# Masks of the prompt scores: from TensorE matmuls to VectorE additions, in the first of two attention stages

## The chip, the cores and the metric

The kernel runs on one core of a Trainium2 chip. The metric is device time of one execution in microseconds, the median of several runs. In what follows TensorE is the matrix engine, VectorE (DVE), ScalarE (ACT) and GpSimd (POOL) are the others that compute, and SyncE (SP) issues most DMAs.

## What is computed

One decoder layer, for a prompt of 1024 tokens and for 8 decode sequences of 8 tokens each. The mixing sub-layer has two head groups: differential attention (4 heads) and NSA, a native sparse attention (8 query heads on 2 key heads, with a compressed, a selected and a window branch). An MLP with squared ReLU follows. At these sizes all 16 blocks of 64 keys are selected in the prompt, so its selected branch is plain causal attention. What matters here is the masked softmax of the prompt:

```python
def masked_softmax(s, mask):
    s = jnp.where(mask, s.astype(jnp.float32), NEG)
    m = jnp.max(s, axis=-1, keepdims=True)
    p = jnp.where(mask, jnp.exp(s - m), 0.0)
    return p / jnp.maximum(jnp.sum(p, axis=-1, keepdims=True), 1e-30)

# nsa_attention: selected and window branches
smask = kpos <= tpos
wmask = (wpos[None, :] >= 0) & (dist >= 0) & (dist < WINDOW)     # WINDOW = 512
# diff_attention
p = masked_softmax(s, kpos[None, :] <= tpos[:, None])
```

## The kernel before

The prompt is cut into 8 tiles of 128 queries, and keys into blocks of 128. The program is one stream of Python calls without loops on the chip. It has these stages in order: input norm and the projections of compressed keys (`stage_keys`), NSA attention of the prompt (`stage_nsa`), differential attention of the prompt with the decode attention in between (`stage_diff`), the output projection, the MLP up and the MLP down.

`scores` (line 397) makes the probabilities of one query tile `i` against the key blocks `kb0` to `i`. Keys 0 to 511 and 512 to 1023 go to separate tiles `S` of 512 columns, one PSUM bank each. Each tile gets two matmuls (line 410), since the queries are split in a high and a low part (`ps`). Where the tile holds the diagonal block, a third matmul adds the diagonal mask (line 417): the identity `identb` in bf16 times the mask `m_diag`, 128 x 128. Where it holds the block at the far end of the window (only window heads, `sw == 1`, and `i >= 4`), another adds `m_far` (line 414). Then VectorE takes the maximum along the row (line 418), and the smaller of two where there are two tiles (line 422); ScalarE makes the exponentials with their sum (line 427). GpSimd scales the probabilities (line 481).

`stage_nsa` runs over 32 jobs: 2 key heads, 8 query tiles and 2 pairs of query heads. A job calls `scores` four times, twice for the selected and twice for the window branch (`nsa_scores`). In `nsa_values`, TensorE transposes the probabilities (line 517) into a PSUM tile `T`, which is copied to `pt` in SBUF, and multiplies them with the values (line 502). `merge` interleaves three lists by their stated costs: the values of the job before, the scores of this job, and fill work, which is the projections of later tiles (line 337). `stage_diff` is built in the same way, over 4 heads and 8 tiles, and calls the same `scores`.

In PSUM the NSA stage has four buffers for `S`, two for `T`, one for the output `o` and one for projections `M` (`PS_N`).

`evac` (line 141) chooses the engine of each copy from `T` to `pt`. `self.ld` holds an account of work in ns, `ld[0]` for ScalarE and `ld[1]` for VectorE. A copy of `n` columns would add 0.83 n + 60 to the first or 1.04 n + 70 to the second, and goes where the account is then lower. `scores` and other functions enter their own work in it. So line 139 (`act_copy`) is the copy on ScalarE and line 150 the one on VectorE. Semaphores and the final order of each engine's instructions are made by the tile framework at the end of the build.

Of the kernel before, what the change touches and what calls it, by code (L numbers as in the profile page):

```python
# [26 lines left out]
P = 128  # L27
# [40 lines left out]
def merge(*lists):  # L68

    lists = [l for l in lists if l]  # L70
    tot = [sum(c for c, _ in l) + 1e-9 for l in lists]
    done = [0.0] * len(lists)
    pos = [0] * len(lists)
    while True:
        best = None
        for n, l in enumerate(lists):
            if pos[n] < len(l):
                f = (done[n] + 0.5 * l[pos[n]][0]) / tot[n]
                if best is None or f < best[0]:
                    best = (f, n)  # L80
        if best is None:
            return
        n = best[1]
        c, fn = lists[n][pos[n]]
        fn()
        done[n] += c
        pos[n] += 1


def interleave(*lists):  # L90

    out = []
    merge(*[[(c, lambda i=i: out.append(i)) for i in l for c in [i[0]]] for l in lists])
    return out
# [31 lines left out]
class Kern:  # L126
# [270 lines left out]
    def scores(self, qs, j, kst, kc, i, kb0, sums, far):  # L397


        nc = self.nc  # L400
        segs = [(a, b) for a, b in ((kb0, min(i + 1, 4)), (max(kb0, 4), i + 1)) if a < b]
        nm = self.sm.tile([P, 2], F32, name="nm", bufs=8)
        tiles = []
        for n, (a, b) in enumerate(segs):
            hf = a // 4
            S = self.psum_s()
            lo = hf * 512
            far_here, diag_here = far and a <= kb0 < b, a <= i < b
            for ps in range(2):
                nc.tensor.matmul(S[:, a * P - lo:b * P - lo], qs[:, ps, j, :],  # L410
                                 kst[hf][:, kc, a * P - lo:b * P - lo],
                                 start=ps == 0, stop=ps == 1 and not (far_here or diag_here))
            if far_here:
                nc.tensor.matmul(S[:, kb0 * P - lo:(kb0 + 1) * P - lo], self.identb, self.m_far, start=False,
                                 stop=not diag_here)
            if diag_here:
                nc.tensor.matmul(S[:, i * P - lo:(i + 1) * P - lo], self.identb, self.m_diag, start=False, stop=True)  # L417
            nc.vector.reduce_max(nm[:, n:n + 1], S[:, a * P - lo:b * P - lo], axis=AX.X, negate=True)  # L418
            tiles.append(S)
            self.ld[1] += 1.04 * (b - a) * P + 66  # L420
        if len(segs) == 2:
            nc.vector.tensor_tensor(nm[:, 0:1], nm[:, 0:1], nm[:, 1:2], op=OP.min)  # L422
            self.ld[1] += 70
        p = self.pp.tile([P, 1024], F32, name="p")
        for n, (a, b) in enumerate(segs):
            lo = a // 4 * 512
            nc.scalar.activation(p[:, a * P:b * P], tiles[n][:, a * P - lo:b * P - lo], AF.Exp, bias=nm[:, 0:1],  # L427
                                 accum_out=sums[:, n:n + 1])
            self.ld[0] += 0.83 * (b - a) * P + 236
        return p  # L430
# [1349 lines left out]
    def fill_nsa(self):  # L1780
        self.kvs = [self.kv0, None]
        fill = self.nfill = Fill()
        sts = {}
        jobs = []
        late = []
        key = None
        kv1 = []
        for g in range(2):
            box = []
            fill.add([(0, lambda g=g, box=box: box.append(self.unit_q(g)))])  # L1790
            for t in [NT] + list(range(NT)) if g == 0 else list(range(NT)) + [NT]:
                st = sts[g, t] = {"g": g}
                items = self.lazy(lambda t=t, st=st, box=box: box[0](t, st), [660.0] * 4 + [10, 224])
                fill.add(interleave(items[:4], late))
                if key:
                    fill.mark(key)
                fill.add(items[4:5])
                late = items[5:]
                key = None
                if g == 0:  # L1800
                    kv1.append((t, self.lazy(lambda t=t: self.kv1_tile(t), [650.0] * 4 + [120])))
                    if t == 0:
                        fill.mark("pre")
                        fill.add([(0, self.kv1_open)])
                    if 1 < t < NT:
                        for _ in range(2 if t < 5 else 1):
                            fill.add(kv1.pop(0)[1])
                if t < NT:
                    late.append((110, lambda g=g, t=t: self.nsa_cmp_scores(g, t, sts[g, t])))
                    key = (g, t)  # L1810
                    jobs += [(g, t, 0), (g, t, 1)]
        fill.add(late)
        self.njobs, self.nsts = jobs, sts

    def stage_nsa(self):
        fill, jobs, sts = self.nfill, self.njobs, self.nsts
        prev = []
        merge(self.klate[:2])
        merge(fill.take(0, (0, 0)), self.klate[2:3])
        for n, (g, t, pr) in enumerate(jobs):  # L1820
            sc = self.nsa_scores(g, t, pr, sts[g, t])
            if n == 2:
                self.consts_late(self.bp)
            if n == 0:
                merge(sc, self.klate[3:])
                sc = []
            nxt = jobs[n + 1] if n + 1 < len(jobs) else None
            key = (nxt[0], nxt[1]) if nxt and nxt[2] == 0 else None
            bud = fill.left() / (len(jobs) - n)
            merge(prev, sc, fill.take(bud, key))  # L1830
            prev = self.nsa_values(g, t, pr, sts[g, t])
        self.tail = prev

    def stage_diff(self):
        fill = Fill()
        sts = {}
        jobs = []
        late = []
        heads = []
        for h in range(4):  # L1840
            weights, tile = self.unit_diff(h)
            for n, t in enumerate([NT] + list(range(NT))):
                st = sts[h, t] = {}
                items = self.lazy(lambda t=t, st=st, tile=tile: tile(t, st), [163.0 * 4] * 6 + [10, 224])
                if n == 0:
                    fill.add([(0, weights)])
                fill.add(interleave(items[:6], late + self.dec_slot(h, n)))
                fill.add(items[6:7])
                if jobs and late:
                    fill.mark(jobs[-1])  # L1850
                late = items[7:]
                if t < NT:
                    jobs.append((h, t))
        fill.add(late)
        fill.mark(jobs[-1])
        for n in range(36, 40):
            fill.add(self.dec_nsa_slot(n))
        prev = self.tail
        merge(prev, fill.take(0, (0, 0)))
        prev = []  # L1860
        for n, (h, t) in enumerate(jobs):
            sc = self.diff_scores(h, t, sts[h, t])
            key = jobs[n + 1] if n + 1 < len(jobs) else None
            bud = fill.left() / (len(jobs) - n)
            merge(prev, sc, fill.take(bud, key))
            prev = self.diff_values(h, t, sts[h, t])
        merge(prev, fill.take(1e12))
# [175 lines left out]
```

## Time and profile before

| | us |
|---|---|
| median of 3 runs | 1824.03 |
| lowest and highest | 1822.09, 1831.58 |
| the profiled execution | 1819.73 |
| its span, first to last instruction | 1817.9 |
| NSA stage of the prompt in it | about 172 to 545 |
| TensorE busy over the span | 1709.6 (94%) |
| VectorE busy | 1137.8 (63%) |
| ScalarE busy | 865.4 (48%) |

The profile is one execution, 4.3 us below the median of the runs. Durations and waits are read from it. Matmul rows overlap, and their ends are modelled, so a sum of their durations is more than the time that they take from the queue; the distance between two starts is what counts. A wait that is put down to an engine tells which semaphore came last. Masks in the NSA stage are the rows of lines 414 and 417 with `S<-maskb,identb`.

### The profile page before, as it was taken

How to read it: one execution, taken by the hardware profiler on the slowest of the kernel's cores; microseconds unless marked ns; L12 is line 12 of the kernel's file. 1: busy time of each engine (PE TensorE's matmuls, PEld its weight loads, DVE VectorE, ACT ScalarE, POOL GpSimd, SP SyncE). 2: the span in 40 equal slices, each digit the busy share in tenths (PEclk: the TensorE clock that was granted, in tenths of full speed). 3: DMA queues.
4: the chain of work that ended last, by engine and by line, in shares of the span. 5: the costliest groups of instructions: out<-in, count | busy, mean ns of one | idle time of the engine just before them, and what ended most of it. 6: DMA issues, size and time to landing. Idle time of an engine off the chain costs nothing. (4 is left out here: it accounts for less than half of the span.)

```text
span 1817.9 us, 33390 instructions
## 1 busy us (share of the span) xinstructions
PE 1709.6 (94%) x12155; PEld 1487.3 (82%) x12155; DVE 1137.8 (63%) x2716; ACT 865.4 (48%) x2188; POOL 273.3 (15%) x517
## 2 busy tenths in 40 slices
PE   7689999999998999999989997999999899999997
PEld 7678776677666778787877877999999899999996
DVE  5357667767863575667665478566666456847665
ACT  5244446456762364555555355444444334543442
POOL 1133335334330121212110000000000000000000
PEclk9888899999998999999998998999999999999999
DMA  7531000000203243424245322434443465554334
GB/s 195 115 75 45 14 14 24 7 4 23 58 7 113 86 145 88 120 81 130 65 134 182 129 91 80 140 133 151 145 145 110 159 214 168 177 165 115 106 118 150
DMA packets 193919, 191.92 MB, mean 106 GB/s; under 512 B 32562, under 2 KB 152986, under 8 KB 193754
## 3 DMA queue, kind: packets, MB, share of 16 engines
q1 hardware_dynamic: 191114, 185.10, 33.2%
q10 hardware_dynamic: 2640, 4.68, 0.8%
q8 instruction: 96, 1.57, 0.4%
q14 instruction: 69, 0.57, 0.1%
HBM read 133.75 MB, written 55.97 MB: 104 GB/s over the span
## 5 line engine op out<-in xcount | busy, mean ns | idle before, releaser
L337 PE MATMUL M<-w,xt 128*128 128x384 f32 (+4 forms) x1584 | 293.4, 330 | 15.4 <-ACT natk L139 12.6
L1665 PE MATMUL Dn<-hf,wf 128*128 128x272 f32 x2304 | 292.4, 290 | 10.1 <-ACT hf L139 8.1
L1665 PEld LDWEIGHTS Dn<-hf,wf 128*128 128x128 f32 x2304 | 291.0, 190 | 11.4 <-ACT hf L139 8.4
L337 PEld LDWEIGHTS M<-w,xt 128*128 128x128 f32 (+1 forms) x1584 | 243.8, 191 | 30.2 <-ACT natk L139 13.5
L427 ACT ACTIVATE p<-S,nm 128x512 f32<-128x512 f32 (+3 forms) x288 | 159.9, 561 | 87.8 <-DVE nm L422 48.8
L418 DVE TENSOR_REDUCE nm<-S 128x1 f32<-128x512 f32 (+3 forms) x288 | 148.1, 527 | 59.1 <-PE S L417 39.3
L175 POOL TENSOR_TENSOR rs_r<-rs_t,mhalf 128x1 f32<-128x1 f32 (+2 forms) x64 | 38.2, 599 | 955.1 <-DVE rs_t L173 952.2
L410 PE MATMUL S<-kst,qs 128*128 128x512 f32 (+3 forms) x576 | 162.1, 373 | 9.6 <-ACT p L427 8.6
L481 POOL TENSOR_SCALAR p<-p,coef 128x640 f32<-128x640 f32 (+7 forms) x128 | 92.5, 736 | 150.5 <-DVE coef L478 66.0
L410 PEld LDWEIGHTS S<-kst,qs 128*128 128x128 f32 x576 | 93.8, 194 | 22.6 <-ACT p L427 11.8
L1363 DVE TENSOR_TENSOR us<-ur,us 128x512 fp32r<-128x512 f32 x96 | 66.1, 691 | 66.2 <-ACT us L139 66.1
L139 ACT ACTIVATE us<-ur 128x512 fp32r<-128x512 f32 x101 | 63.4, 629 | 82.3 <-PE Uc L1437 50.4
L1437 PE MATMUL Ub<-xc,us 128*128 128x272 f32 x744 | 101.0, 288 | 0.0
L139 ACT ACTIVATE wf<-q 128x512 fp32r<-128x512 f32 x69 | 43.6, 632 | 116.5 <-PE Dn L1665 108.8
L1437 PE MATMUL Ua<-xc,us 128*128 128x272 f32 x744 | 99.0, 289 | 0.0
L150 DVE COPY pt<-T 128x512 f32<-128x512 f32 (+3 forms) x100 | 61.7, 618 | 55.9 <-PE T L517 42.1
L1437 PEld LDWEIGHTS Ub<-xc,us 128*128 128x128 f32 x744 | 96.1, 188 | 0.0
L1437 PEld LDWEIGHTS Ua<-xc,us 128*128 128x128 f32 x744 | 95.8, 189 | 0.0
L139 ACT ACTIVATE hf<-hr 128x544 fp32r<-128x544 f32 (+1 forms) x127 | 74.9, 590 | 43.8 <-PE Dn L1675 28.1
L139 ACT ACTIVATE pt<-T 128x512 f32<-128x512 f32 (+4 forms) x116 | 60.8, 527 | 69.0 <-PE T L517 41.1
L1363 DVE TENSOR_TENSOR hf<-hr,hf 128x544 fp32r<-128x544 f32 (+1 forms) x127 | 82.0, 648 | 16.0 <-ACT hf L139 15.8
L517 PEld LDWEIGHTS T<-ident,p 128*128 128x128 f32 x528 | 56.5, 141 | 40.7 <-issue 34.6
(363 smaller groups left out, 3351.0 us busy)
## 6 DMA issues: line engine op xcount, KB each, us to landing
hF<-uh SPq DMA_DIRECT2D x105, 272.0 KB
hr<-hF SPq DMA_DIRECT2D x92, 272.0 KB
kvp<-cache_diff_kv SPq DMA_DIRECT2D x128, 128.0 KB
ur<-w_up SPq DMA_DIRECT2D x32, 512.0 KB
q<-w_down SPq DMA_DIRECT2D x13, 1024.0 KB
raw<-w_in SPq DMA_DIRECT2D x32, 192.0 KB
raw<-w_in SPq DMA_DIRECT2D x40, 128.0 KB
hr<-hF SPq DMA_DIRECT2D x32, 136.0 KB
```

What stands on the lines that cost most here:

```text
L139: self.nc.scalar.activation(out, in_, AF.Copy, scale=scale)
L150: self.nc.vector.tensor_copy(out, in_)
L175: nc.gpsimd.tensor_tensor(r[:rows], t[:rows], self.mhalf[:rows], op=OP.pow)
L337: nc.tensor.matmul(ps[1][:m, :n], self.xt[c][:, a, k, c0:c0 + m], ws[k][:, b, :n], start=i == 0, stop=i == len(ops) - 1)
L410: nc.tensor.matmul(S[:, a * P - lo:b * P - lo], qs[:, ps, j, :], kst[hf][:, kc, a * P - lo:b * P - lo], start=ps == 0, stop=ps == 1 and no ...
L418: nc.vector.reduce_max(nm[:, n:n + 1], S[:, a * P - lo:b * P - lo], axis=AX.X, negate=True)
L427: nc.scalar.activation(p[:, a * P:b * P], tiles[n][:, a * P - lo:b * P - lo], AF.Exp, bias=nm[:, 0:1], accum_out=sums[:, n:n + 1])
L481: nc.gpsimd.tensor_scalar(v, v, coef[:, sw + 1, j:j + 1], 0.0, op0=OP.mult, op1=OP.add)
L517: nc.tensor.transpose(T[:, m * 256 + jj * P:m * 256 + jj * P + P], st["p", sw, pr * 2 + jj][:, kb * P:(kb + 1) * P], self.ident)
L1363: lo.tensor_sub(w[:, 1], src, f32(w[:, 0]))
L1437: nc.tensor.matmul(ps[:, p, :QT], w[:, a, k, :], x[:, b, k, :], start=start and cnt == 0, stop=cnt == 11, skip_group_check=True)
L1665: nc.tensor.matmul(dps[db][:, q, :QT], w[:, a, db * P:(db + 1) * P], h[:, b, q * QT:(q + 1) * QT], start=st and m == 0, stop=sp and m == 2)
```

## The change

In the NSA stage the two mask matmuls of a score tile are replaced by additions on VectorE, in place in PSUM, between the score matmuls and the maximum. The second score matmul then ends the accumulation. Each addition enters 240 in VectorE's account. `mask_dve` is set at the end of `fill_nsa`, before any score of the NSA stage is made, and cleared at the start of `stage_diff`, where masks stay matmuls. The masks of the compressed branch (line 437) and of the decode attention stay as they are.

```diff
@@ def scores
+            pe = not self.mask_dve
             for ps in range(2):
                 nc.tensor.matmul(S[:, a * P - lo:b * P - lo], qs[:, ps, j, :],
                                  kst[hf][:, kc, a * P - lo:b * P - lo],
-                                 start=ps == 0, stop=ps == 1 and not (far_here or diag_here))
-            if far_here:
+                                 start=ps == 0, stop=ps == 1 and not (pe and (far_here or diag_here)))
+            if far_here and pe:
                 nc.tensor.matmul(S[:, kb0 * P - lo:(kb0 + 1) * P - lo], self.identb, self.m_far, start=False,
                                  stop=not diag_here)
-            if diag_here:
+            if diag_here and pe:
                 nc.tensor.matmul(S[:, i * P - lo:(i + 1) * P - lo], self.identb, self.m_diag, start=False, stop=True)
+            for here, kb, mask in ((far_here, kb0, self.m_far), (diag_here, i, self.m_diag)):
+                if here and not pe:
+                    v = S[:, kb * P - lo:(kb + 1) * P - lo]
+                    nc.vector.tensor_add(v, v, mask)
+                    self.ld[1] += 240
             nc.vector.reduce_max(nm[:, n:n + 1], S[:, a * P - lo:b * P - lo], axis=AX.X, negate=True)
@@ def fill_nsa
         self.njobs, self.nsts = jobs, sts
+        self.mask_dve = True
@@ def stage_diff
+        self.mask_dve = False
         fill = Fill()
```

## Rows read from the trace of the kernel before

**Rows 1.** Busy us (and count) by stretch: PE, PEld, DVE, ACT, POOL; clock, DMA.

```profile
172.00:545.00 373.00, 362.69 (x2498) 259.26 (x2499) 260.05 (x797) 207.90 (x684) 137.86 (x224) 0.98 0.08 20
...
172.00:200.00 28.00, 22.59 (x131) 20.59 (x132) 19.75 (x64) 11.79 (x52) 9.32 (x18) 0.70 0.09 25
...
545.00:600.00 55.00, 48.66 (x278) 34.04 (x276) 18.19 (x64) 13.08 (x34) 5.71 (x14) 0.91 0.38 114
...
1200.00:1818.00 618.00, 592.67 (x4702) 590.05 (x4700) 380.50 (x604) 261.67 (x453) 6.34 (x10) 0.98 0.45 148
```

**Rows 2.** Waits of TensorE, 172 to 545: us in total, times, longest.

```profile
PE S L441 <- ACT qs L139: 2.6, 2, 1.8
...
PE S L410 <- ACT p L427: 1.9, 2, 1.4
PE o L502 <- DVE pt L150: 1.3, 1, 1.3
```

**Rows 3.** Mask matmuls by line, 172 to 545: count, busy us, mean ns, idle.

```profile
L417 PE MATMUL S<-maskb,identb 128*128 128x128 bf16 x128 | 29.8, 233 | 0.0
...
L414 PE MATMUL S<-maskb,identb 128*128 128x128 bf16 x32 | 7.4, 230 | 0.0
```

**Rows 4.** TensorE timeline at four score tiles: start us, us, what.

```profile
313.08 0.39 PE L410 MATMUL S<-kst,qs 128*128 128x512 f32 x1
313.31 0.29 PE L337 MATMUL M<-w,xt 128*128 128x280 f32 x1
...
438.55 0.40 PE L410 MATMUL S<-kst,qs 128*128 128x512 f32 x1
438.79 0.23 PE L417 MATMUL S<-maskb,identb 128*128 128x128 bf16 x1
438.83 0.36 PE L337 MATMUL M<-w,xt 128*128 128x256 f32 x1
...
446.61 0.40 PE L410 MATMUL S<-kst,qs 128*128 128x512 f32 x1
446.94 0.44 PE L502 MATMUL o<-pt,vst 128*64 128x256 f32 x2
...
444.17 0.40 PE L410 MATMUL S<-kst,qs 128*128 128x512 f32 x1
444.41 0.23 PE L417 MATMUL S<-maskb,identb 128*128 128x128 bf16 x1
444.57 0.44 PE L502 MATMUL o<-pt,vst 128*64 128x256 f32 x2
```

**Rows 5.** VectorE groups by form, 172 to 545: count, busy us, mean ns, idle.

```profile
L418 DVE TENSOR_REDUCE nm<-S 128x1 f32<-128x512 f32 x72 | 48.8, 683 | 15.2 <-PE S L410 7.4 <-PE S L417 6.2 <-PE S L414 1.0
...
L418 DVE TENSOR_REDUCE nm<-S 128x1 f32<-128x128 f32 x40 | 11.0, 280 | 3.3 <-PE S L414 1.9 <-PE S L417 1.2
...
L545 DVE TENSOR_TENSOR pt<-o,pt 64x512 f32<-64x512 f32 x15 | 10.1, 674 | 1.5 <-ACT pt L139 1.5
...
L356 DVE TENSOR_TENSOR rope<-nat,cos 128x128 f32<-128x128 f32 x14 | 5.9, 422 | 0.0
...
L360 DVE TENSOR_TENSOR nat<-rope,rope 128x128 f32<-128x128 f32 x14 | 4.4, 318 | 0.0
```

**Rows 6.** VectorE timeline, a dependent pair: start us, us, what.

```profile
420.20 0.16 DVE L451 RECIPROCAL coef<-coef 128x4 f32<-128x4 f32 x1
...
420.40 0.16 DVE L452 TENSOR_TENSOR coef<-coef,gates 128x4 f32<-128x4 f32 x1
```

**Rows 7.** Copies of transposed probabilities by form on either engine, 172 to 545.

```profile
L150 DVE COPY pt<-T 128x512 f32<-128x512 f32 x73 | 50.2, 688 | 37.4 <-PE T L517 33.1 <-DMA mixT<-pt 1.9 <-PE o L502 1.0
...
L139 ACT ACTIVATE pt<-T 128x512 f32<-128x512 f32 x49 | 29.3, 598 | 36.5 <-PE T L517 33.6 <-DVE coef L478 1.6 <-PE o L502 0.9
```

**Rows 8.** Busy us by stretch, as in rows 1.

```profile
400.00:450.00 50.00, 50.00 (x354) 35.24 (x354) 35.95 (x113) 29.90 (x105) 20.59 (x39) 1.00 0.04 9
450.00:500.00 50.00, 50.00 (x347) 33.10 (x346) 40.98 (x123) 35.84 (x117) 17.34 (x22) 1.00 0.25 64
```

## The prediction

> **What bounds the kernel now.** I read the windows of the trace by stage first. The diff sets its flag for the first attention stage alone, the stretch from 172 to 545 us [rows 1]. TensorE is busy there for 362.7 of 373 us, VectorE for 260, ScalarE for 208; the granted clock is 0.98 over the stretch, so nearly all of it ran at the upper level, 2.4 GHz. The next view is the waits of TensorE in that stretch. Its longest waits are 2.6, 1.9 and 1.3 us in all for three of the causes [rows 2], and all its idle time is 373.0 - 362.7 = 10.3 us. Nothing holds TensorE up for long: its queue is the pace of the stage, and VectorE has 113 us to spare. The chain of waits on the page says nothing here, since it breaks off at the last instructions.
>
> A busy matmul row can hide a slow stream, because rows of neighbours overlap. So I read starts, not durations, in the TensorE timeline: whether work taken out of its queue brings the next matmul forward. That is the step on which the sum rests.
>
> **What is removed.** The stage holds 128 diagonal masks (line 417) and 32 far masks (line 414), 160 matmuls in all, each with its own weight load [rows 3]. A row of such a matmul lasts 230 to 233 ns, but most of that lies under its neighbours. What one costs is seen by comparing two score tiles of the same width [rows 4]. Without a mask, a projection matmul starts 313.31 - 313.08 = 0.23 us after the second score matmul; with one, 438.83 - 438.55 = 0.28. Ahead of a value matmul the two are 446.94 - 446.61 = 0.33 and 444.57 - 444.17 = 0.40. So a mask costs TensorE 0.05 or 0.07 us, by what follows it. I went through the masked tiles between 200 and 545 us in this way: about half are followed by a projection or another score matmul, the rest by value matmuls and transposes, which behave like the second pair. The sum is 80 x 0.05 + 80 x 0.07 = 9.6 us; I use 10, since the tiles before 200 us run at a lower clock (0.70 from 172 to 200 us, [rows 1]). The bounds are 160 x 0.05 = 8 and 160 x 0.07 = 11.2 us.
>
> The Trainium skill, in the page "TensorE: Matmul & The Clock Gate", section "Back-to-back issue gap", gives about 81 ns per matmul for a sustained stream of load and matmul pairs at 128 columns. By that figure the saving would be an estimated 160 x 0.081 = 13.0 us, 3 us more than here; the starts above are lower, and they decide.
>
> **What is added.** VectorE gets 160 additions of 128 x 128, one operand and the result in PSUM, the other operand the bf16 mask. No row of before shows this form. From below the nearest is the reduction of a 128 x 128 score tile, 280 ns (it only reads PSUM); from above the rope product of the same size, 422 ns; the rope sum takes 318, and the one addition here with a PSUM operand takes 674 ns for 512 columns [rows 5]. The reductions of 512 and of 128 columns differ by 683 - 280 = 403 ns; taking that off the last one gives 674 - 403 = 271 ns. I take 300 ns, nearest to the two that touch PSUM. The reduction that follows must wait for the result. How long that takes shows in a dependent pair: the reciprocal at 420.20 ends at 420.36 and its product starts at 420.40 [rows 6]. So an addition takes about 300 + 40 = 340 ns of VectorE's time, 160 x 0.34 = 54 us in the stage, between 160 x 0.31 = 50 (from the 271 ns) and 160 x 0.46 = 74 (from the 422).
>
> **What moves.** Each addition also enters 240 ns into VectorE's account, 38.4 us in all, and evac gives each copy out of PSUM to the engine with the lower account. A copy of 512 columns counts 602 on VectorE and 485 on ScalarE, so 38,400 / 1,087 = 35 copies change sides. By their rows (688 ns on VectorE, 598 on ScalarE, [rows 7]) VectorE gives up 24 us and ScalarE takes on 21. VectorE goes from 260 to 260 + 54 - 24 = 290 us of 373, ScalarE from 208 to 229. Both still fit. No DMA is added or moved; the mask stays in SBUF for the other heads.
>
> **What waits where.** The addition takes over the wait for the score matmul that the reduction had, so no new engine enters the chain. The wait ends earlier by the mask's share, and the maximum comes later by 0.34 us less that, about 0.3. Behind the addition in VectorE's queue stand the reduction, the exponentials that need it (ScalarE), and the copies of transposed probabilities, which TensorE's value matmuls and the two transpose buffers need. Of four score buffers each now comes back about 0.3 us later, plus what the fuller VectorE queue adds. The cover is the order of the work: the values of one job run beside the scores of the next. How thin it is shows in TensorE's waits for ScalarE's exponentials (1.9 us) and for copies (1.3 us) [rows 2]. VectorE's free time falls from 113 to 83 us, and its queue is fuller in the dense stretch from 450 to 500 us, where it has 41.0 of 50 us now [rows 8]. I put the new stalls at 5 us, an estimate: half of the 10.3 us that TensorE is idle now. The bounds are 0, if the buffers cover everything, and 10.3, if all idle time doubles. Less than 0 I leave out for the stalls, since no edit makes any of these buffers come free earlier relative to the matmuls that wait for it.
>
> **Where the gain goes.** After 545 us TensorE is busy 48.7 of 55 us while the cache pages are read, and in the last stage 592.7 of 618 [rows 1]. The loads of both follow the end of this stage, so an earlier end carries through. The account of the copies starts the next stage level either way.
>
> **The sum.** 10 - 5 = 5 us gained. The profiled execution took 1819.7 us, of which the span is 1817.9, and would take 1814.7. The median of the runs shown is 1824.0, 4.3 above it; from there the forecast is **1819 us**.
>
> **The rivals.** *Full gain.* The four score buffers and two transpose buffers cover the later maxima; nothing new stalls. For it: VectorE would have 83 us free, and TensorE's waits are short. Against it: the dense stretch. It gives 1824 - 10 = 1814, between 1812.8 and 1816.
>
> *TensorE is not the pace.* Its busy time is overstated, and what is taken out of its queue becomes idle time. For it: weight loads fill 259.3 of 373 us here (70%), and 590 of 618 (95%) in the last stage [rows 1]. Against it: the next matmul starts at once behind a mask [rows 4], and there are few waits [rows 2]. It gives no change, 1824, between 1820 and 1828. The Trainium skill, page "Perfetto Trace Analysis", section "Identifying the Most-Contended Engine", holds that matmul busy share is a poor measure of how near the engine is to its limit, and that the share of weight loads is a better one; by that rule this rival would be the likelier, and the starts in this trace speak against it.
>
> *VectorE becomes the pace.* In the stretch from 450 to 500 us VectorE has 41.0 of 50 us [rows 8]. At the stage's mean of 160 / 373 = 0.43 masks a us, 21 additions bring 7.3 us and take 3.2 away in copies: 45.1 of 50, or 90%. An engine in strict order that also waits for two others can hardly be fuller. This decides from the point where VectorE's free time in a stretch is less than the waits that it has anyway. If that holds over half of the stage, 80 additions lengthen it by 80 x (0.34 - 0.15) = 15 us, the other half gains 5, and the end is at 1834, between 1829 and 1840. Against it: from 400 to 450 us VectorE has 36.0 of 50 [rows 8], so the queue can recover between dense stretches.
>
> **How the numbers follow.** Forecast 0.47, full gain 0.22, TensorE not the pace 0.20, VectorE the pace 0.11. About 0.5% (9.1 us) is what a measurement of this kernel can tell from no change; it puts the border at 1814.9 and 1833.1. Three quarters of the full gain lie below, 0.17. VectorE as pace counts as slower, 0.11, though its lower end is inside. The rest, 0.72, is no change. The range reaches from 1812, the lower end of the full gain, to 1830, the top of the case in which nothing is gained with the spread of the runs before (1822.1 to 1831.6); outside are most of the last rival and a little on either side. The forecast's own range is 1815 to 1823.
>
> **What would show it.** Right: the rows of lines 414 and 417 in this stage are gone, 160 additions of about 300 ns stand there, copies of transposed tiles go from VectorE to ScalarE (about 35), the stage ends near 540 us, and TensorE's waits for the exponentials and copies grow by a few us. Wrong in price: additions well over 400 ns, or a mask that cost TensorE more than 0.07 us. Wrong in kind: TensorE's idle time in the stage grows by 10 us or more, or the scheduler puts the streams in another order, so that the stages after 545 us change in length, which nothing in this trace can exclude.

## The result, and the profile after

The kernel after takes **1837.96 us** (median of 5 runs, 1833.32 to 1839.91), the kernel before 1825.13 beside it (1822.09 to 1832.01). The ratio is **1.0066 [1.0048, 1.0085]**: slower by about 12 us, where 1819 was forecast. The profiled execution of after took 1835.25 us, with a span of 1833.5.

Most of the first attention stage looks as the prediction described it. The window of after that answers to the first of [rows 1]:

```profile
172.00:545.00 373.00, 356.09 (x2346) 253.90 (x2345) 271.94 (x909) 226.21 (x721) 131.67 (x217) 0.97 0.08 19
```

VectorE's busy time rises from 260.1 to 271.9 us and ScalarE's from 207.9 to 226.2, TensorE's falls from 362.7 to 356.1. (After runs 5.7 us ahead by then, so the two windows don't hold quite the same work.) The groups by form of the same stretch, which answer to [rows 5] and [rows 7]:

```profile
L139 ACT ACTIVATE pt<-T 128x512 f32<-128x512 f32 x80 | 47.2, 598 | 41.2 <-PE T L523 39.3 <-PE o L508 0.9 <-DMA mixT<-pt 0.2
L422 DVE TENSOR_TENSOR S<-S,maskb 128x128 f32<-128x128 f32 x159 | 45.0, 291 | 21.7 <-PE S L411 18.7 <-ACT pt L139 0.6 <-PE T L523 0.6
L150 DVE COPY pt<-T 128x512 f32<-128x512 f32 x44 | 30.2, 686 | 22.7 <-PE T L523 18.7 <-PE o L508 3.1 <-PE S L411 0.7
```

An addition takes 291 ns, and 31 copies more run on ScalarE (80, [rows 7] had 49). So far the terms hold. I cut the two traces at events: the ends of the first and of the last of the 16 additions `pt<-o,pt` (line 551, 545 before), with which the first stage hands over its values, and the last copy of a transposed prompt output `ot` in the second stage. The columns are those of [rows 1]; first before, first and second stage, then after.

```profile
211.10:558.70 347.60, 341.40 (x2359) 235.22 (x2357) 238.06 (x719) 195.25 (x624) 124.90 (x197) 1.00 0.07 19
558.70:999.90 441.20, 418.75 (x2833) 343.07 (x2834) 271.75 (x850) 221.42 (x662) 74.23 (x159) 0.97 0.39 117
```

```profile
205.00:553.30 348.30, 335.39 (x2208) 232.93 (x2207) 249.88 (x824) 211.83 (x659) 122.26 (x195) 0.98 0.07 19
553.30:1011.90 458.60, 427.87 (x2833) 347.40 (x2834) 271.03 (x850) 220.93 (x662) 73.64 (x159) 0.96 0.38 113
```

The first stage is as long as it was (348.3 against 347.6 us), but not by standing still. TensorE's idle time in it rises from 6.2 to 12.9 us, and the granted clock falls from 1.00 to 0.98. The wait for exponentials that [rows 2] shows at 1.9 us is now

```profile
PE S L411 <- ACT p L433: 5.4, 7, 2.4
```

and at three places the clock fell to the lower level (0.50, 1.2 GHz) behind waits of TensorE: one of 2.4 us that ended at 273.2, one of 1.2 us that ended at 308.7, and two of 1.3 and 0.7 us that ended at 337.5 and 339.3. The windows around them in after:

```profile
272.00:284.00 12.00, 9.95 (x45) 7.43 (x46) 9.80 (x39) 7.92 (x26) 5.03 (x6) 0.72 0.04 11
308.00:316.00 8.00, 7.26 (x42) 4.62 (x42) 6.39 (x22) 6.76 (x19) 6.48 (x10) 0.79 0.06 16
336.00:344.00 8.00, 5.83 (x25) 4.17 (x24) 5.72 (x19) 5.28 (x15) 3.56 (x4) 0.79 0.06 16
```

They cost 0.28 x 12 + 0.21 x 8 + 0.21 x 8 = 6.7 us of full clock. Before has two waits, 1.9 us in all, at the first of these places, and its clock stayed at 1.00 in this stage.

The second stage, whose code the diff leaves alone and which has the same 2833 matmuls and the same busy time on VectorE and on ScalarE, is **17.4 us longer** in these two executions. Ahead of the windows after is 6.1 us earlier, of which 5.7 were there when the last matmuls of the compressed keys started (164.80 against 170.46 us), before any TensorE instruction stands in another place: that isn't the change's. Behind them after is 3.6 us longer (821.6 against 818.0). TensorE's idle time in the second stage rises from 22.5 to 30.7 us; the other 9 us are longer matmul rows, at a granted clock of 0.96 in place of 0.97.

Not all of the 17.4 us is the order's. x3 below runs the second stage in the order of before, and in its profiled execution it took 452.7 us at a clock of 0.95:

```profile
556.30:1009.00 452.70, 427.07 (x2833) 349.31 (x2834) 271.85 (x850) 222.12 (x662) 74.36 (x159) 0.95 0.38 114
```

Two readings are steadier. TensorE's idle time in the second stage is 21.7 to 25.6 us in the nine traces with the old order there (u2 nearly so), and 28.9 to 34.7 us in the five that were laid out with after's balance (after, x2, x4, x6, u1). And the length times the granted clock, an estimate of what the stage would take at the upper level, is 427 to 432 us in the nine and 440 to 444 in the five. So some 12 us go with the order, the rest with the clock. TensorE's waits there, in us in all, times, longest; before, then after:

```profile
PE S L410 <- ACT p L427: 6.7, 3, 3.3
```

```profile
PE S L411 <- ACT p L433: 6.5, 4, 4.1
...
PE T L571 <- DVE nm L428: 2.9, 1, 2.9
...
PE T L571 <- DVE jk L569: 1.9, 2, 1.3
```

No single wait makes the loss. There are more short ones, such as the transpose of a normalised output (line 571), which now stands in TensorE's queue ahead of the VectorE work that it needs. That is what another order of the same work looks like. Setting the two built programs side by side shows that the order is another: the planner that lays out each engine's stream at build time put 1524 of the 2991 TensorE instructions written ahead of the second stage, and 1638 of the 2244 of that stage, in other places. (The expectations below count on into the output projection: 1950 of 3335.)

### The profile page after: what moved, and what is told of

The parts are those of the page before. It is cut to its first block, busy times and chain, and to the rows that moved or that the text cites. A ratio compares the mean times of both kernels' runs of the same rounds, so it can differ in the third digit from the quotient of the medians.

```text
span 1833.5 us, 33297 instructions
## 1 busy us (share of the span) xinstructions
PE 1711.0 (93%) x11995; PEld 1486.7 (81%) x11995; DVE 1150.2 (63%) x2836; ACT 884.3 (48%) x2228; POOL 271.9 (15%) x517
## 5 line engine op out<-in xcount | busy, mean ns | idle before, releaser
L1671 PE MATMUL Dn<-hf,wf 128*128 128x272 f32 x2304 | 294.1, 290 | 11.5 <-ACT hf L139 7.8
L337 PE MATMUL M<-w,xt 128*128 128x384 f32 (+4 forms) x1584 | 287.2, 328 | 13.6 <-ACT natk L139 10.2
L337 PEld LDWEIGHTS M<-w,xt 128*128 128x128 f32 (+1 forms) x1584 | 245.5, 190 | 29.0 <-ACT natk L139 11.2
L411 PE MATMUL S<-kst,qs 128*128 128x512 f32 (+3 forms) x576 | 160.7, 377 | 14.1 <-ACT p L433 11.9
L139 ACT ACTIVATE pt<-T 128x512 f32<-128x512 f32 (+4 forms) x156 | 80.8, 530 | 83.8 <-PE T L523 49.9
L523 PE MATMUL T<-ident,p 128*128 128x128 f32 x528 | 89.6, 288 | 2.7 <-POOL p L487 1.8
```

Source lines behind the costliest of these rows:

```text
L139: self.nc.scalar.activation(out, in_, AF.Copy, scale=scale)
L337: nc.tensor.matmul(ps[1][:m, :n], self.xt[c][:, a, k, c0:c0 + m], ws[k][:, b, :n], start=i == 0, stop=i == len(ops) - 1)
L523: nc.tensor.transpose(T[:, m * 256 + jj * P:m * 256 + jj * P + P], st["p", sw, pr * 2 + jj][:, kb * P:(kb + 1) * P], self.ident)
L1671: nc.tensor.matmul(dps[db][:, q, :QT], w[:, a, db * P:(db + 1) * P], h[:, b, q * QT:(q + 1) * QT], start=st and m == 0, stop=sp and m == 2)
```

## The experiments

Three theories. **Order**: the new layout of the streams costs the time, and the change itself is worth about what was predicted. **VectorE**: the additions and the waits behind them cost more than the matmuls give back. **Account**: the copies moved to ScalarE lengthen the loop. To separate them, most kernels below are built twice. The first build gives an order; in the second, each instruction gets an edge without a semaphore to the one ahead of it on its engine in that order, in short:

```diff
+for name in order_of_the_other_build:      # by place in the trace
+    i = by_name[name]
+    if i.engine in last:
+        tc.add_manual_dep(i, last[i.engine], NoSync)
+    last[i.engine] = name
```

Where it is laid on, every engine's stream is that of the other kernel, apart from masks and the copies' engines. Ratios are against the kernel before, run beside it on the same chip, with 95% intervals; 0.1% is 1.8 us. The diffs show the change in short; masks and additions are touched where `mask_dve` is set, in the first stage.

### The parts of the change, in the old order

**x1**: the kernel after in the order of before, without the account entry.

```diff
                     nc.vector.tensor_add(v, v, mask)
-                    self.ld[1] += 240
```

> The kernel after, but every engine gets the order of the kernel before, instruction by instruction (each addition stands right before the maximum that reads it), and nothing is charged to the account, so that all copies stay on their engines. Only the direct effect of the change is left. Order theory (the loss came from the new order in which the build put everything, the change itself is worth the predicted -5 us): 1816 to 1823 us. VectorE theory (the additions and the waits behind them cost more than 160 matmuls give back): 1832 to 1840 us.

Measured: 1.0008 [0.9990, 1.0025], 1823.99 us. Just outside the order theory's numbers and far from the VectorE theory's: no gain, and no loss.

**x8**: the kernel before in its own order, without the masks of the first stage.

```diff
-                nc.tensor.matmul(S[:, kb0 * P - lo:(kb0 + 1) * P - lo], self.identb, self.m_far, start=False,
-                                 stop=not diag_here)
-                nc.tensor.matmul(S[:, i * P - lo:(i + 1) * P - lo], self.identb, self.m_diag, start=False, stop=True)
```

> The kernel before in its own order, with the 160 mask matmuls of the first attention stage left out and nothing in their place: prompt scores of that stage are unmasked. The prediction's term for TensorE: 10 us less, 1811 to 1815 us; then the additions must have cost as much in the run with additions in the old order. If the matmuls lay in TensorE's slack: 1820 to 1825 us, and then neither mattered.

Measured: 0.9936 [0.9913, 0.9959], 11.7 us less (1814.64). The matmuls do cost TensorE about what the prediction said. In the trace the first stage takes 339.7 us, 7.9 less than before.

**x9**: the kernel before in its own order, with the additions beside the mask matmuls.

```diff
+                    nc.vector.tensor_add(v, v, mask)
```

> The kernel before in its own order with its mask matmuls, and the additions as well, each right before its maximum (the mask is put on twice). Only VectorE's side of the change. The prediction's term: 5 us more, 1826 to 1832 us. By the two runs in the old order (no masks, and additions in place of matmuls) the additions cost 13 us: 1834 to 1841 us.

Measured: 1.0065 [1.0041, 1.0088], 11.9 us more. So additions that stand right before their maximum cost about 12 us, which agrees with x1 less x8 (0.72%), and not 5. Its windows, first and second stage:

```profile
214.40:569.40 355.00, 345.74 (x2359) 236.83 (x2357) 276.43 (x864) 196.84 (x624) 124.81 (x197) 0.99 0.07 19
569.40:1014.80 445.40, 422.33 (x2833) 345.88 (x2834) 272.25 (x849) 221.80 (x662) 74.14 (x159) 0.96 0.39 116
```

In this one execution the first stage is 7.4 us longer than before: 3.1 us more idle time of TensorE, and 4.3 us more in matmul rows, at a granted clock of 0.99 in place of 1.00. The second stage has the old order and is 4.2 us longer, at 0.96 in place of 0.97; other executions of that order differ by more (x3).

**x5**: the kernel before in its own order, with the account entry alone.

```diff
+                    self.ld[1] += 240
```

> The kernel before with its mask matmuls and its order; only the account is charged, so that 40 copies of transposed scores run on ScalarE in place of VectorE, each at the place that it had. Account theory (these copies cost the time, whatever the order): 1838 to 1846 us, as the run with account and new order. Order theory: 1821 to 1828 us.

Measured: 1.0007 [0.9992, 1.0023], 1827.47 us, as the order theory said. Here 86 copies of the first stage change engine, 40 of them net to ScalarE, and 32 of the second, 16 each way, since the account is left at another balance. At their old places they cost nothing: the account theory falls.

**y1**: the kernel after in the order of before, with the account put back to before's at the second stage.

```diff
     def stage_diff(self):
         self.mask_dve = False
+        self.ld = [158954.24, 159152.64]
```

> Additions and the 40 moved copies together in the order of the kernel before, the second stage unchanged (its account reset). Against the run with additions alone in the old order (1.0008) it tells what the moved copies do for the additions. If the additions cost their 13 us (0.08% minus the -0.64% without masks) because VectorE is full: the 40 copies make room and the time falls to 1812 to 1818 us. If they cost it because the wait in front of the maximum grows at the place where they stand: 1821 to 1827 us as without the moved copies.

Measured: 1.0023 [1.0004, 1.0042], 1830.09 us, above both ranges. The moved copies don't make the additions cheaper, which speaks against a full VectorE as what makes them dear. That it is the wait in front of the maximum instead is argued: no run varies that wait alone.

### The order

**x2**: the kernel before, with the account entry, in the order of after; each mask matmul stands right behind its score matmul.

```diff
+                    self.ld[1] += 240
```

> The kernel before with its mask matmuls, but the account is charged as in the kernel after (the same 40 copies go to ScalarE) and every engine gets the order of the kernel after. No addition on VectorE. Order theory (order and moved copies together): slower than before by 13 to 20 us, 1838 to 1845 us, and the second attention stage as long as in the kernel after (458 us from the last fold to the last output, against 441). VectorE theory: as before within 3 us, 1822 to 1828 us.

**x6**: the kernel before, line for line, in the order of after.

> The kernel before with its mask matmuls and all copies on their engines; only the order is that of the kernel after, on every engine. Order theory: 1838 to 1846 us. Account theory: 1820 to 1827 us. If each bears a part, this run and the run with the copies alone add up to the +23 us of both together.

Measured: x2 1.0139 [1.0116, 1.0162], x6 **1.0133** [1.0101, 1.0165]. In x6 nothing but the order differs from the kernel before: same instructions, same engines, 24 us more. Its first stage took 356.6 us in the trace (347.6 before) and its second 466.0. That is the order theory, above the numbers that it gave (x2 1846.3 us, x6 1851.39), and more than the whole loss of the kernel after. The kernel after has the order of x2 and its copies on the same engines; only masks differ, and it stands at 1.0066 (beside its own runs of before). So in that order the swap of matmuls for additions gains 0.7%, where in the order of before it gains nothing (x1): what the change is worth hangs on the order around it.

**x3**: the kernel after without the account entry; the planner is free.

```diff
-                    self.ld[1] += 240
```

> The kernel after without the 240 ns that are charged to VectorE's account for an addition: all copies stay on the engines that they had before, the order is the build's own. Account theory (the copies moved to ScalarE lengthen the loop): 1816 to 1823 us. VectorE theory: 1834 to 1842 us, since the additions stay and VectorE has 40 copies more. Order theory: like the kernel with the old order, give or take what a new order happens to cost, 1816 to 1838 us.

Measured: 1.0032 [1.0012, 1.0053], 1826.70 us, in the order theory's range alone. The first stage gets another order, while the second keeps the old one: the 24 instructions of TensorE that stand elsewhere do so where the two stages meet.

**x4**: the kernel before with the account entry; the planner is free.

```diff
+                    self.ld[1] += 240
```

> The kernel before with its mask matmuls, but VectorE's account is charged 240 ns for each mask as in the kernel after; the order is the build's own. Account theory: 1835 to 1842 us. Order theory: the order changes as much as it did in the kernel after, so the time may be anywhere in 1820 to 1842 us, and a second attention stage of another length than 441 us would show it. VectorE theory: 1823 to 1828 us.

Measured: 1.0129 [1.0109, 1.0149], 1843.55 us, a little above every range. An account entry without any addition costs 23 us, while the copies that it moves cost nothing in the old order (x5). So it acts through the layout. In its trace the first stage takes 361 us and the second 453.7. Why the new layouts of the first stage suit mask matmuls so badly, and additions well, I haven't found; that stays open. Nor was one engine's new order run beside the old order of the others, so which engine's layout carries the loss isn't known.

### Why the second stage has another order

**x7**: the kernel after; from `stage_diff` on, the order and the account's value of before.

```diff
+        self.ld = [158954.24, 159152.64]
```

> The kernel after through its first attention stage (additions, account, order); from the first instruction of the second attention stage on, the engines get the order of the kernel before and the account its value there, so that the copies of that stage are on their old engines too. Order theory, with the loss in the second stage: 1818 to 1826 us, the second stage back from 459 to 441 us. If something left behind by the first stage lengthens the second: 1834 to 1842 us, second stage 455 us and more.

Measured: 0.9992 [0.9971, 1.0013], 1822.72 us, second stage 444.4 us. Nothing that the first stage leaves behind in memory or queues lengthens the second; its order does, with the engines of its copies, which by themselves cost nothing in x5. Only the account is left as the way by which the change reaches that far: x3 makes no entry in it, and the planner lays out the second stage as before. At the start of `stage_diff` ScalarE's side is 198 ns behind VectorE's in the kernel before and 112 ns ahead in the kernel after. That difference of 310 ns turns round the choice of 32 copies, and the planner lays out the stage around them.

**u1**: the kernel before with after's balance at that point; the planner is free.

```diff
     def stage_diff(self):
+        self.ld = [176227.84, 176115.84]
```

> The kernel before with one line more: where the second attention stage begins, the account is set to the balance that it has there in the kernel after (ScalarE 112 ns ahead of VectorE, where the kernel before has it 198 ns behind). The first attention stage is the kernel before's, instruction by instruction; in the second, 32 copies change engine (16 each way) and the build lays its instructions in other places. Hand-over theory (this balance alone makes the loss): 1838 to 1848 us, second stage 455 us and more. If the loss needs the new first stage: 1821 to 1828 us.

**u2**: the kernel after with before's balance there; the planner is free.

```diff
     def stage_diff(self):
         self.mask_dve = False
+        self.ld = [158954.24, 159152.64]
```

> The kernel after with one line more: where the second attention stage begins, the account is set to the balance that it has there in the kernel before. Nothing else is forced; the build then lays the second stage nearly as in the kernel before by itself (50 of 3335 TensorE instructions stand elsewhere, against 1950 in the kernel after). Hand-over theory: 1817 to 1825 us. Otherwise: 1834 to 1842 us.

Measured: u1 **1.0055** [1.0032, 1.0077], u2 **0.9980** [0.9961, 1.0000]. Second stage of u1, then of u2:

```profile
562.90:1016.70 453.80, 422.90 (x2833) 344.81 (x2834) 271.89 (x850) 220.66 (x662) 73.78 (x159) 0.97 0.38 114
```

```profile
558.40:1000.30 441.90, 420.20 (x2833) 344.79 (x2834) 271.95 (x849) 221.71 (x662) 74.13 (x159) 0.97 0.39 117
```

One line that only sets two numbers of the account adds 10 us to the kernel before (1836.07 us, between the two ranges that were stated); the same line the other way takes 0.86%, 16 us, from the kernel after, each measured beside its own runs of before. It isn't the clock: the granted clock is 0.97 in both second stages, and the 12 runs of u1 have a mean of 0.9671, the 31 of before beside them 0.9669. TensorE is idle for 30.9 us of the stage in u1 and for 21.7 in u2. Its longest waits in u1's second stage show the transpose again (line 585 there is 571 of after):

```profile
PE S L420 <- ACT p L447: 8.5, 8, 4.0
PE T L585 <- DVE nm L442: 5.0, 1, 5.0
```

### Is the old order special, or is each balance a draw?

**v1** to **v4**: the kernel after with another balance `d` there, -800, -400, 200 and 600 ns; the planner is free.

```diff
     def stage_diff(self):
         self.mask_dve = False
+        self.ld = [159000 + d, 159000]
```

> The kernel after, with ScalarE 800 ns behind VectorE in the account where the second stage begins (before: 198 behind, after: 112 ahead). The first stage is the kernel after's; in the second, 38 copies and 1399 TensorE instructions stand otherwise than with 198 behind. Draw theory (each balance lays another order, worth its own time): anywhere in 1818 to 1842 us. Old-order theory (only the kernel before's order is good): 1834 to 1842 us. Sign theory (ScalarE behind is good, ahead is bad): 1818 to 1826 us.

> The same with ScalarE 400 ns behind: 16 copies and 1768 TensorE instructions stand otherwise than with 198 behind. Draw theory: 1818 to 1842 us, and not the time of the others of its sign. Old-order theory: 1834 to 1842 us. Sign theory: 1818 to 1826 us.

> The same with ScalarE 200 ns ahead: 9 copies and 304 TensorE instructions stand otherwise than with 198 behind, the least of all balances looked at, though the sign is the kernel after's. Draw theory and old-order theory: 1818 to 1828 us, since nearly all stands as in the kernel before. Sign theory: 1834 to 1842 us.

> The same with ScalarE 600 ns ahead: 34 copies and 1235 TensorE instructions stand otherwise than with 198 behind. Draw theory: 1818 to 1842 us. Old-order theory and sign theory: 1834 to 1842 us.

Measured, with u2 and the kernel after in their places; the last two columns are the second stage in the profiled execution, its length and granted clock:

| ScalarE's side, ns | ratio to before | us | clock |
|---|---|---|---|
| -800 (v1) | 1.0003 [0.9985, 1.0021] | 446.1 | 0.96 |
| -400 (v2) | 1.0025 [1.0009, 1.0042] | 448.1 | 0.96 |
| -198 (u2) | 0.9980 [0.9961, 1.0000] | 441.9 | 0.97 |
| +112 (after) | 1.0066 [1.0048, 1.0085] | 458.6 | 0.96 |
| +200 (v3) | 1.0035 [1.0017, 1.0054] | 452.9 | 0.95 |
| +600 (v4) | 0.9996 [0.9977, 1.0016] | 444.1 | 0.97 |

The sign doesn't decide (+600 is as good as -800), and v1 and v4, with 1399 and 1235 instructions in other places, aren't slow, so the old order isn't the only good one. v3, nearest to the old order with 304, is slower than both, and at 1831.13 us outside what any theory gave for it: nearness doesn't help either. Each balance is a draw, between -0.2 and +0.7% with the same change in the first stage, and the kernel after drew the worst of the six, though its interval meets that of v3. The mean of the six is +0.18%. The first stage takes 347 to 348 us in all six traces, and the length of the second puts them in the same sequence as the timed ratios do: the difference arises there. Times the clock, after's second stage is 440 us and the other five 428 to 431, so between those five the traces show little but the clock.

## Why the prediction was wrong

**What bounds the kernel: right.** Taking 160 matmuls out of TensorE's queue shortens the run (x8), so the rival "TensorE is not the pace" is out. The Trainium skill's page "Perfetto Trace Analysis", section "Identifying the Most-Contended Engine", counts the share of weight loads among the better measures of how near TensorE is to its limit; here it was 70% [rows 1], and TensorE's queue was the pace all the same.

**What is removed: right.** 10 us, between 8 and 11.2, from the distances between starts [rows 4]; x8 measures 11.7 [7.5, 15.9]. The pairs alone would not have carried it: before other projection matmuls the distance behind a score matmul of 512 columns is 0.23 to 0.32 us without a mask and 0.27 to 0.28 with one, so the 0.05 us is one pair of a wide spread, and x8 is what confirms the term. The estimate of 13.0 us from the Trainium skill's page "TensorE: Matmul & The Clock Gate", section "Back-to-back issue gap", lies inside that interval as well.

**What is added: right.** 300 ns forecast, 291 measured.

**What moves: right in count, wrong in reach.** 35 copies were forecast, 31 more stand on ScalarE in the window, 40 over the run, and by themselves they cost nothing (x5).

**What waits where: mis-sized.** The term of 5 us, with bounds of 0 and 10.3, measures 11.9 [7.5, 16.1] by x9, with the additions right before their maximum. Half the idle time was a guess at how thin the cover is, and the clock had no term. Of the 11.9 us the clock could hold half: the granted clock of the 8 runs of x9 is 0.9634 on average, that of the 31 of before beside them 0.9669, and 0.0035 / 0.9669 x 1825 us is 6.6 us. That is argued, not shown; v1 and v4 have as low a mean clock (0.9633 and 0.9632, against 0.9670) and aren't slower than before.

Where the planner may place the additions itself, the change in its own stage does better: u2, with the second stage back to nearly the old order, stands at -0.20%, 3.6 us less, and 0.43% below y1 beside it; x7, with exactly the old order there, stands at -0.08% [-0.29, 0.13]. Neither is clear of zero; a gain of 5 us lies inside the interval of u2 and at the end of that of x7.

The windows of before and after show what became of the term. In the first stage TensorE's idle time grew by 6.7 us, near the 5 that were forecast. The busy time fell by 6.0 us; without the 6.7 us that the clock cost it would have fallen by 12.7, which is near x8's 11.7 (an estimate, as if all of that cost lay in busy time). So it is -12.7 + 6.7 + 6.7 = +0.7 us: the term that the sum lacks is the clock behind the new waits. The falls aren't an accident of one execution: v1, v2, v4, u2 and x7, whose first stage is after's, all show 0.98 there, v3 0.99, and u1, whose first stage is before's, 1.00 (it takes 350.1 us there).

**Where the gain goes: the step that failed.** "The account of the copies starts the next stage level either way." It starts within 310 ns of level, and that isn't the same: the choice between two engines turns on the sign of a small difference, the planner on those choices, and the second stage takes 17 us longer in the trace, some 12 of them by the order. By the timed runs the loss is this: -0.20% for the change in its own stage (u2), +0.86% for the hand-over (after less u2), together +0.66%; with x7 in place of u2 the parts are -0.08 and +0.74%. On the kernel before the hand-over alone costs 0.55% (u1). The last paragraph of the prediction names another order of later stages as what would make it wrong, but gives it no chance. The six balances above say how wide such a case is: about 0.9% from best to worst, more than the whole of what the change itself can bring (0.64%, x8).

**VectorE becomes the pace: the right place on the scale, not the mechanism.** That rival gave 1834, between 1829 and 1840, and the time lies there. But VectorE is busy for 249.9 of 348.3 us in the first stage of after, y1 with fewer copies on it isn't faster than x1 (1.0023 against 1.0008), and the stage that got longer has no more VectorE work than before.

No kernel here is clearly faster than the kernel before with the masks kept; u2 touches 1.0000 with the end of its interval.

## What to carry to other kernels

Where a planner lays out the streams, or a running balance chooses engines, an edit acts on all that is built after it; its price is its own work plus a new draw of the order, and here the draws lay 0.9% apart, while the edit in its own stage gained 0.1 or 0.2%, neither clear of zero. Build the change once more with the old order laid on the engines, and once with the running state put back at the next stage, before a gain or loss of a per cent is put down to the operation that was changed. And take a step such as "the next stage starts as before" for what it is, a statement about a state, which can be read from the two builds. Where an edit adds waits to an engine whose queue is the pace, give the clock a term of its own: here it took as much as the waits.

## What the runs showed of the hardware

The granted clock of one and the same sequence isn't the same in each execution. x8 and x1 have the same order and instructions in the second stage. After a stretch in which TensorE had one wait of 0.5 us (in the first window below of each, where it is busy for 3.53 of 4 us), its clock fell in x8 to the lower level (0.50, 1.2 GHz, in the window from 878) and stayed up in x1. Windows of 4 us, columns as in [rows 1]; x8, then x1, at the same place of the stage:

```profile
870.00:874.00 4.00, 3.53 (x29) 2.73 (x27) 3.11 (x12) 2.20 (x6) 1.20 (x3) 1.00 0.16 45
874.00:878.00 4.00, 4.00 (x23) 3.56 (x22) 1.85 (x10) 1.55 (x7) 0.74 (x2) 0.72 0.39 111
878.00:882.00 4.00, 4.00 (x18) 3.50 (x18) 1.67 (x6) 1.85 (x5) 0.11 (x1) 0.50 0.58 167
882.00:886.00 4.00, 4.00 (x25) 3.51 (x23) 2.47 (x7) 1.25 (x4) 0.29 (x1) 0.93 0.01 2
```

```profile
861.00:865.00 4.00, 3.53 (x27) 2.76 (x26) 2.28 (x8) 2.49 (x8) 1.20 (x3) 1.00 0.08 23
865.00:869.00 4.00, 4.00 (x30) 3.47 (x29) 2.24 (x12) 1.58 (x7) 0.17 (x2) 1.00 0.36 103
869.00:873.00 4.00, 4.00 (x31) 3.59 (x30) 2.50 (x10) 2.56 (x8) 0.68 (x1) 1.00 0.62 177
```

Behind the wait, x8's windows start 23, 18 and 25 matmuls, x1's 30 and 31: about 3.4 us of full clock lost ((0.28 + 0.50 + 0.07) x 4 us), of the 8.0 us by which the second stage of x8's execution (449.9 us) is longer than x1's (441.9). Between before and x3 the same order differs by 11.5 us (441.2 and 452.7, at 0.97 and 0.95). So the length of a stage in a single profile of this kernel can't tell a change of 8 to 11 us from no change; the idle time of TensorE beside it, and the clock, say more. The runs of the kernel before show the same in the large: among the 31 beside u1 the lowest mean clock, 0.963, went with 1826.5 us and the highest, 0.971, with 1815.5 and 1818.5. What decides between the two I can't tell from these traces.
